# Summing the squares of the value products with one matmul: fold to 64 partitions, stack rounded part and remainder

## The chip, the cores and the metric

The kernel runs on one core of a Trainium2 chip. The metric is the device time of one execution in microseconds (us), the median of several. The engines are TensorE (PE; its weight loads are PEld), VectorE (DVE), ScalarE (ACT), GpSimd (POOL) and SyncE (SP), which here only issues transfers.

## The reference, cut to what matters

The reference is a two-layer decoder trunk on 1024 tokens of width 1024. Layer 0 is a retention mixer, layer 1 differential attention with 16 heads. What the change touches is the end of layer 1: the attention output of each head, 128 wide, gets an RMS norm over those 128 values.

```python
attn = probs[:, :, 0] - lam * probs[:, :, 1]
...
out = rmsnorm(out, subln_g, eps=GN_EPS) * (1.0 - lambda_init)
y = out.transpose(0, 2, 1, 3).reshape(B, S, D_INNER)
gated = jax.nn.silu(g.astype(jnp.float32)) * y
return gated.astype(w_out.dtype) @ w_out
```

So for each head and each token the sum of 128 squares is needed. 

## The kernel before, in words

**Precision.** Every large matmul works on a rounded part (type fp32r) and a remainder, so a product is three matmuls: high x high, high x low, low x high. ACT rounds (a cast) and DVE or POOL subtracts to get the remainder.

**Layer 1.** `attention_layer` goes through 16 heads and, in each, through 8 blocks of 128 queries in the order 6, 2, 3, 7, 4, 0, 1, 5: 128 steps. In a step PE makes the logits of the next block (L752, L755). DVE finds row maxima (L780, L782, L783), ACT takes exponentials (L785), and DVE combines the two softmaxes into A (L788, L789, L791). PE transposes A (L809), ACT casts it (L812), DVE subtracts for the remainder (L813). After every second block, `values` multiplies V with the transposed weights of two blocks (L823 to L825) into one half of a PSUM bank `ob`: 128 partitions are the head's 128 value dimensions, 256 columns are two blocks of queries. There are 16 x 4 = 64 such value products.

**The squares.** Behind each value product ACT squares it (L831) and casts the square (L832), DVE subtracts for the remainder (L833), and a further DVE instruction makes the gated product `go` (L837 or L839). Later `square_sum` issues the transfer of `go` (L844), lets PE sum over partitions with a matrix of ones, once for the rounded part and once for the remainder (L845, L846), into the other half of the bank, and stores row 0 of it (L848, L849). The bank has one buffer. When a batch of heads (0 to 7, 8 to 11, 12 to 15) is complete, `row_scales` reads the sums back and makes the norm's factors; `finish` multiplies them into the stored products on POOL (L733) in later steps, for the first two batches.

**What sets the order.** PE's order is the program's order (a manual schedule). To fill PE's waits, the projections of later heads come as a generator, `filler`, in steps of about 0.65 us, and a counter `clk["pe"]` adds up estimated PE time. `fill_until(t)` pulls filler up to a time, with allowances from `SLACK` for what the other engines must do in between; `fill_total` spreads the filler over the steps, so its total is fixed. `ready_o` is the point after which a square sum may be issued: the counter after the value product plus `SLACK["sq"]`. It is issued in the next step, behind that step's transposes; at the end of the first two batches it is issued in the same step; after the last value product there is no filler left. ACT, DVE and POOL take their instructions from a list scheduler that goes by priority and by estimated readiness; the softmax, the casts of the transposes and the squares have raised priority. On the chip each of these engines runs its list in order. POOL also subtracts for the remainders of the weights (L83 and, for some of the output weights, L94).

Of the kernel before, what the change touches and what calls it, by code (L numbers as in the profile page):

```python
# [10 lines left out]
F32 = mybir.dt.float32  # L11
F32R = mybir.dt.float32r
I32 = mybir.dt.int32
AF = mybir.ActivationFunctionType
# [5 lines left out]
P = 128  # L20
# [8 lines left out]
NE = 16  # L29
NEG = -1.0e30  # L30
PRIO = 600
SLACK = {'base': 3.4, 'wide': 4.4, 'turn': 2.0, 'av': 1.6, 'sq': 2.0, 'qk': 1.2}
START_T = (("T", 1), ("R", 1))
MXB = 1
AHEAD = 2
# [11 lines left out]
def _f32(ap):  # L47
    return ap.bitcast(F32)


class _Trunk:
# [523 lines left out]
    def attention_layer(self, HR, QR, pmm, ws0, slots):  # L575
        nc, io = self.nc, self.io
        with ExitStack() as es:
# [8 lines left out]
            wk = self.pool(es, "l1w")  # L586
# [10 lines left out]
            def v_(h, kb, lo):  # L597
                return QR[:, 10 + 2 * (h % 3) + lo, kb * P:(kb + 1) * P]

            L, U = slice(0, 64), slice(64, 128)  # L600
# [96 lines left out]
            def fill_until(t):  # L697
                while clk["pe"] < t and pull():
                    pass
# [5 lines left out]
            def need(*key):  # L705
                while key not in done and pull():
                    pass
                assert key in done, key

            def batch(h):  # L710
                return next((b, h - h0, h1 - h0) for b, (h0, h1) in enumerate(BATCHES) if h < h1)
# [103 lines left out]
            def values(h, j):  # L815
                ath, atl = ats.pop((h, j))
                nk = 2 * j + 2
                ob = psm.tile([P, 512], F32, tag="AV", name="ps_o")
                o = ob[:, 0:256]
                for kb in range(nk):  # L820
                    last = kb == nk - 1
                    c0 = P if last else 0
                    nc.tensor.matmul(o[:, c0:], v_(h, kb, 0), ath[:, kb, c0:], start=(kb == 0), stop=False)  # L823
                    nc.tensor.matmul(o[:, c0:], v_(h, kb, 0), atl[:, kb, c0:], start=False, stop=False)
                    nc.tensor.matmul(o[:, c0:], v_(h, kb, 1), ath[:, kb, c0:], start=False, stop=last)  # L825
                clk["pe"] += nk * 0.327
                sq = wk.tile([P, 256], F32, tag="sq", name="sq")
                sqh = wk.tile([P, 256], F32R, tag="sqh", name="sqh")
                sql = wk.tile([P, 256], F32R, tag="sql", name="sql")
                with self.tc.high_priority(offset=PRIO):  # L830
                    nc.scalar.activation(sq, o, AF.Square)  # L831
                    nc.scalar.copy(sqh, sq)  # L832
                    nc.vector.tensor_sub(sql, sq, _f32(sqh))  # L833
                go = wk.tile([P, 256], F32, tag="go", name="go", bufs=2)
                if h < LATE:
                    sg = sgs[h][j // 2][:, (j % 2) * 256:(j % 2) * 256 + 256]
                    nc.vector.scalar_tensor_tensor(go, o, self.subg, sg, op0=ALU.mult, op1=ALU.mult)  # L837
                else:
                    nc.vector.tensor_scalar(go, o, self.subg, None, op0=ALU.mult)  # L839
                return ob, sqh, sql, go  # L840

            def square_sum(h, j, ob, sqh, sql, go):
                b, hh, nh = batch(h)
                nc.scalar.dma_start(self.g1r[b][2 * j:2 * j + 2, :, hh, :].rearrange("t p q -> p t q"), go.rearrange("p (t q) -> p t q", t=2))  # L844
                nc.tensor.matmul(ob[:, 256:512], self.ones, sqh, start=True, stop=False)  # L845
                nc.tensor.matmul(ob[:, 256:512], self.ones, sql, start=False, stop=True)  # L846
                ssr = wk.tile([1, 256], F32, tag="ssr", name="ssr")
                nc.vector.tensor_copy(ssr, ob[0:1, 256:512])  # L848
                nc.scalar.dma_start(self.ssd[b][2 * j:2 * j + 2, hh:hh + 1, :].rearrange("t a q -> a t q"), ssr.rearrange("a (t q) -> a t q", t=2))  # L849
# [34 lines left out]
            for s, (h, i) in enumerate(seq):  # L884
# [4 lines left out]
                if nxt is not None:  # L889
# [3 lines left out]
                    need("qk", seq[min(s + AHEAD, len(seq) - 1)][0])  # L893
                    fill_until(ready - SLACK["qk"])
                    Ss = logits(*nxt)
                    nready = clk["pe"] + SLACK["base"] + SLACK["wide"] * (nxt[1] + 1) / 8.0
                fill_until(ready)
# [12 lines left out]
                if i >= 4:  # L910
                    fill_until(t_done + SLACK["turn"])
                    attn_t(h, i, A, 1)
# [4 lines left out]
                if pend is not None:  # L917
                    fill_until(ready_o)
                    square_sum(*pend)
                    pend = None  # L920
                if i % 2 == 1:
                    need("v", h // 2)
                    if h < LATE:
                        need("g", h)
                    fill_until(t_done + SLACK["av"])
                    pend = (h, i // 2) + values(h, i // 2)
                    ready_o = clk["pe"] + SLACK["sq"]
                    if i == ORDER[-1] and h + 1 in (BATCHES[0][1], BATCHES[1][1]):
# [11 lines left out]
            if pend is not None:  # L940
                square_sum(*pend)
# [140 lines left out]
```

## Time and profile before

| | |
|---|---|
| median of three runs | 2182.5 us (2181.49 to 2183.46) |
| the profiled execution's own time | 2179.38 us |
| its span, first to last instruction | 2177.6 us |
| mean granted clock of TensorE | 0.997 |
| instructions | 31046 |

The page of the profile gives each engine's busy time over the span, then groups of instructions by line. A group's row has the number of instructions, the busy time, the mean duration and the idle time of the engine just in front of them with what ended it. A timeline row has the start, the duration, the engine and line, the operation and the tiles it writes and reads, and in brackets the idle time in front of it and its releaser. [...]

### The profile page before, as it was taken

The numbers are of one execution on the slowest core, as the hardware profiler recorded it, in microseconds if no ns is written. First come the engines' busy times: TensorE is split into PE (matmuls) and PEld (weight loads), VectorE is DVE, ScalarE is ACT, GpSimd is POOL, SyncE is SP. The second block draws the span as 40 slices with busy tenths as digits, with TensorE's granted clock in tenths as the row PEclk, the third lists the DMA queues.
The fourth block names the chain that finished last, engine by engine and source line by source line (L and its number), as shares of the span: only waits on it lengthen the run. The fifth ranks groups of instructions, "written<-read, shape, count | busy, mean of one in ns | idle before, by whom it ended". The sixth has DMA issues, their size and how long they took to land.

```text
span 2177.6 us, 31046 instructions
## 1 busy us (share of the span) xinstructions
PE 2132.8 (98%) x11861; PEld 1790.8 (82%) x11861; DVE 1283.4 (59%) x3155; ACT 851.6 (39%) x1638; POOL 429.3 (20%) x246
## 2 busy tenths in 40 slices
PE   8999999999999999999999999999999999999998
PEld 7888988898897888787888888888787878877776
DVE  6254344334437438646777666767766777776644
ACT  4121221122123333335455555554545555554321
POOL 2332501511512000121111111111133111211300
PEclk9999999999999999999999999999999999999999
DMA  4112112111213545311111111111244113334743
GB/s 167 62 39 68 57 39 73 47 54 54 64 57 99 179 155 174 113 48 42 49 37 42 49 40 42 39 38 43 84 135 136 47 38 95 112 104 146 257 150 134
DMA packets 98916, 185.48 MB, mean 85 GB/s; under 512 B 8848, under 2 KB 51024, under 8 KB 98640
## 3 DMA queue, kind: packets, MB, share of 16 engines
q1 hardware_dynamic: 63824, 166.50, 23.6%
q10 hardware_dynamic: 34944, 17.01, 2.6%
q8 instruction: 93, 1.52, 0.3%
q14 instruction: 55, 0.45, 0.1%
HBM read 147.67 MB, written 38.95 MB: 86 GB/s over the span
## 4 chain that ended last, share of the span: by engine, by line
PE 92%; DVE 3%; issue 1%; ACT 1%; DMA 1%; POOL 0%; ACTq 0%; DVEq 0%; POOLq 0%
PE ps_mm L158 6%; PE ps_mm L157 6%; PE ps_mm L159 5%; PE ps_mm L215 5%; PE ps_mm L122 5%; PE ps_mm L124 5%; PE ps_mm L123 5%; PE ps_mm L217 5%; PE ps_mm L216 5%; PE ps_t L809 3%; PE ps_ret L396 3%; PE ps_s L752 3%; PE ps_mm L650 3%; PE ps_mm L651 3%; PE ps_mm L652 3%; PE ps_mm L167 3%
## 5 line engine op out<-in xcount | busy, mean ns | idle before, releaser
L83 POOL TENSOR_TENSOR w_l<-w_raw,w_h 128x1024 fp32r<-128x1024 f32 x112 | 271.2, 2427 | 1168.8 <-ACT w_h L82 1165.3
L785 ACT ACTIVATE e<-ps_s,nm 128x896 f32<-128x896 f32 (+7 forms) x256 | 189.8, 742 | 103.4 <-DVE nm L783 93.8
L215 PE MATMUL ps_mm<-RB,w_h 128*128 128x512 f32 x512 | 209.4, 409 | 0.4 <-ACT RB L150 0.4
L157 PE MATMUL ps_mm<-RA,w_h 128*128 128x512 f32 x512 | 203.9, 398 | 1.2 <-DVE sg L426 1.1
L158 PE MATMUL ps_mm<-RA,w_h 128*128 128x512 f32 x512 | 204.6, 400 | 0.0
L216 PE MATMUL ps_mm<-RB,w_h 128*128 128x512 f32 x512 | 201.9, 394 | 1.0 <-DVE RB L151 1.0
L217 PE MATMUL ps_mm<-RB,w_l 128*128 128x512 f32 x512 | 202.5, 395 | 0.0
L159 PE MATMUL ps_mm<-RA,w_l 128*128 128x512 f32 x512 | 201.9, 395 | 0.0
L812 ACT CAST ath<-ps_t 128x512 fp32r<-128x512 f32 (+1 forms) x192 | 91.9, 479 | 227.0 <-PE ps_t L809 217.5
L780 DVE TENSOR_REDUCE mx<-ps_s 128x1 f32<-128x640 f32 (+2 forms) x192 | 119.5, 622 | 78.7 <-PE ps_s L755 74.4
L82 ACT CAST w_h<-w_raw 128x1024 fp32r<-128x1024 f32 x112 | 117.6, 1050 | 123.2 <-PE ps_mm L158 39.0
L650 PE MATMUL ps_mm<-w_h,RB 128*128 128x256 f32 x512 | 147.4, 288 | 0.0
L169 PE MATMUL ps_mm<-w_h,RA 128*128 128x256 f32 x512 | 146.1, 286 | 0.0
L167 PE MATMUL ps_mm<-w_h,RA 128*128 128x256 f32 x512 | 145.3, 285 | 0.5 <-ACT RA L150 0.5
L168 PE MATMUL ps_mm<-w_l,RA 128*128 128x256 f32 x512 | 145.2, 285 | 0.1
L111 DVE TENSOR_TENSOR g_l<-w_raw,g_h 128x1024 fp32r<-128x1024 f32 x60 | 82.7, 1378 | 105.7 <-ACT g_h L110 105.6
L651 PE MATMUL ps_mm<-w_l,RB 128*128 128x256 f32 x512 | 143.6, 280 | 0.0
L652 PE MATMUL ps_mm<-w_h,RB 128*128 128x256 f32 x512 | 143.6, 280 | 0.0
L110 ACT CAST g_h<-w_raw 128x1024 fp32r<-128x1024 f32 x60 | 63.0, 1051 | 172.2 <-PE ps_mm L123 126.4
L157 PEld LDWEIGHTS ps_mm<-RA,w_h 128*128 128x128 f32 x512 | 96.1, 188 | 24.5 <-DVE sg L426 1.6
L217 PEld LDWEIGHTS ps_mm<-RB,w_l 128*128 128x128 f32 x512 | 96.1, 188 | 23.7
L159 PEld LDWEIGHTS ps_mm<-RA,w_l 128*128 128x128 f32 x512 | 96.2, 188 | 22.3
(211 smaller groups left out, 5392.7 us busy)
## 6 DMA issues: line engine op xcount, KB each, us to landing
w_raw<-in_wn SPq DMA_DIRECT2D x64, 512.0 KB
w_raw<-in_wv SPq DMA_DIRECT2D x32, 512.0 KB
w_raw<-in_wo SPq DMA_DIRECT2D x32, 512.0 KB
w_raw<-g SPq DMA_DIRECT2D x32, 512.0 KB
w_raw<-g1f SPq DMA_DIRECT2D x24, 512.0 KB
xt<-in_x SPq DMA_DIRECT2D x16, 512.0 KB
w_raw<-in_wg SPq DMA_DIRECT2D x16, 512.0 KB
g<-go ACTq DMA_DIRECT2D x32, 256.0 KB
```

Of the source, the lines that this page charges most:

```text
L83: nc.gpsimd.tensor_sub(l, raw, _f32(h))
L157: nc.tensor.matmul(ps, wh[:, k], region[:, kt, cols], start=(kt == 0), stop=False)
L158: nc.tensor.matmul(ps, wh[:, k], region[:, 8 + kt, cols], start=False, stop=False)
L159: nc.tensor.matmul(ps, wl[:, k], region[:, kt, cols], start=False, stop=(kt == KT - 1))
L167: nc.tensor.matmul(ps, region[:, kt, cols], wh[:, k], start=(kt == 0), stop=False)
L215: nc.tensor.matmul(ps, wh[:, k], HR[:, kt, tok], start=(kt == 0), stop=False)
L216: nc.tensor.matmul(ps, wh[:, k], HR[:, 8 + kt, tok], start=False, stop=False)
L217: nc.tensor.matmul(ps, wl[:, k], HR[:, kt, tok], start=False, stop=(kt == KT - 1))
L650: nc.tensor.matmul(ps[:, t, :], HR[:, kt, cols], wh[:, k], start=(kt == 0), stop=False)
L651: nc.tensor.matmul(ps[:, t, :], HR[:, kt, cols], wl[:, k], start=False, stop=False)
L652: nc.tensor.matmul(ps[:, t, :], HR[:, 8 + kt, cols], wh[:, k], start=False, stop=(kt == KT - 1))
L785: nc.scalar.activation(e[:, 0:n], S[:, 0:n], AF.Exp, bias=nm, accum_out=(s0 if m == 0 else s1))
```

## The change

The product's 128 partitions are squared in two instructions of 64 partitions each, the second half into a tile of its own that lies on the first 64 partitions. POOL adds the two halves. ACT casts the 64-partition sum into partitions 0 to 63 of a 128-partition tile `sqs`, and DVE writes the remainder into partitions 64 to 127. One matmul with ones then sums all 128 partitions, rounded part and remainder together. `SLACK["sq"]` goes from 2.0 to 3.2.

```diff
-SLACK = {'base': 3.4, 'wide': 4.4, 'turn': 2.0, 'av': 1.6, 'sq': 2.0, 'qk': 1.2}
+SLACK = {'base': 3.4, 'wide': 4.4, 'turn': 2.0, 'av': 1.6, 'sq': 3.2, 'qk': 1.2}
...
-                sq = wk.tile([P, 256], F32, tag="sq", name="sq")
-                sqh = wk.tile([P, 256], F32R, tag="sqh", name="sqh")
-                sql = wk.tile([P, 256], F32R, tag="sql", name="sql")
+                sq = wk.tile([64, 256], F32, tag="sq", name="sq")
+                sqb = wk.tile([64, 256], F32, tag="sqb", name="sqb")
+                sqs = wk.tile([P, 256], F32R, tag="sqs", name="sqs")
                 with self.tc.high_priority(offset=PRIO):
-                    nc.scalar.activation(sq, o, AF.Square)
-                    nc.scalar.copy(sqh, sq)
-                    nc.vector.tensor_sub(sql, sq, _f32(sqh))
+                    nc.scalar.activation(sq, o[L], AF.Square)
+                    nc.scalar.activation(sqb, o[U], AF.Square)
+                    nc.gpsimd.tensor_add(sq, sq, sqb)
+                    nc.scalar.copy(sqs[L], sq)
+                    nc.vector.tensor_sub(sqs[U], sq, _f32(sqs[L]))
...
-                return ob, sqh, sql, go
-
-            def square_sum(h, j, ob, sqh, sql, go):
+                return ob, sqs, go
+
+            def square_sum(h, j, ob, sqs, go):
...
-                nc.tensor.matmul(ob[:, 256:512], self.ones, sqh, start=True, stop=False)
-                nc.tensor.matmul(ob[:, 256:512], self.ones, sql, start=False, stop=True)
+                nc.tensor.matmul(ob[:, 256:512], self.ones, sqs, start=True, stop=True)
```

`L` and `U` are the partitions 0 to 63 and 64 to 127.

## Rows read from the trace of the kernel before

**Rows 1.** The page, part 1: busy time, share of the span, instructions.

```profile
PE 2132.8 (98%) x11861; PEld 1790.8 (82%) x11861; DVE 1283.4 (59%) x3155; ACT 851.6 (39%) x1638; POOL 429.3 (20%) x246
```

**Rows 2.** Busy time by stretch: length, PE, PEld, DVE, ACT, POOL, clock, DMA share, GB/s.

```profile
980.00:2003.00 1023.00, 1003.31 (x5915) 837.87 (x5913) 728.76 (x1932) 535.87 (x1147) 176.17 (x83) 1.00 0.22 67
```

**Rows 3.** PE's waits from 980 to 2010: total us, times, longest.

```profile
PE ps_t L809 <- DVE e L791: 4.1, 5, 2.0
```

**Rows 4.** Timeline, DVE and PE: first and last tight transposes of 14.

```profile
1050.89 1.28 DVE L791 SCALAR_TENSOR_TENSOR e<-e,arr 128x1024 f32<-128x1024 f32 x1
...
1052.40 0.60 PE L809 MATMUL ps_t<-ident,e 128*128 128x128 f32 x4
...
1994.50 1.02 DVE L791 SCALAR_TENSOR_TENSOR e<-e,arr 128x768 f32<-128x768 f32 x1
...
1995.80 0.60 PE L809 MATMUL ps_t<-ident,e 128*128 128x128 f32 x4
```

**Rows 5.** Timeline of PE around one square sum.

```profile
1316.10 0.37 PE L845 MATMUL ps_o<-sqh,ones 128*128 128x256 f32 x1
1316.30 0.28 PE L846 MATMUL ps_o<-sql,ones 128*128 128x256 f32 x1
1316.42 0.28 PE L650 MATMUL ps_mm<-w_h,RB 128*128 128x256 f32 x1
```

**Rows 6.** Timeline of ACT, DVE and PE from one Square to the next transposes.

```profile
1570.37 0.59 ACT L223 ACTIVATE RA<-ps_mm 64x512 fp32r<-64x512 f32 x1
1570.99 0.39 ACT L831 ACTIVATE sq<-ps_o 128x256 f32<-128x256 f32 x1
...
1571.27 1.11 ACT L785 ACTIVATE e<-ps_s,nm 128x1024 f32<-128x1024 f32 x1
...
1572.36 0.41 ACT L832 CAST sqh<-sq 128x256 fp32r<-128x256 f32 x1
...
1573.47 1.29 DVE L791 SCALAR_TENSOR_TENSOR e<-e,arr 128x1024 f32<-128x1024 f32 x1
...
1574.90 0.63 PE L809 MATMUL ps_t<-ident,e 128*128 128x128 f32 x4 [0.80 <-DVE e L791]
...
1575.56 0.59 ACT L812 CAST ath<-ps_t 128x512 fp32r<-128x512 f32 x1 [2.79 <-PE ps_t L809]
```

**Rows 7.** Timeline of ACT: first and last of 13 exponentials between Square and cast.

```profile
1014.86 0.89 ACT L785 ACTIVATE e<-ps_s,nm 128x768 f32<-128x768 f32 x1
...
1992.46 0.90 ACT L785 ACTIVATE e<-ps_s,nm 128x768 f32<-128x768 f32 x1
```

**Rows 8.** Waits of ACT and DVE from 980 to 2010.

```profile
ACT e L785 <- DVE sql L833: 3.7, 7, 0.5
...
DVE go L837 <- ACT sq L831: 24.8, 29, 2.4
```

**Rows 9.** Groups by line, POOL: count, busy us, mean ns, idle before, releasers.

```profile
L83 POOL TENSOR_TENSOR w_l<-w_raw,w_h 128x1024 fp32r<-128x1024 f32 x112 | 271.2, 2427 | 1168.8 <-ACT w_h L82 1165.3 <-PE ps_t L147 3.1
```

**Rows 10.** One line of layer 0, POOL: ns min/median/max, first and last start.

```profile
L314 POOL TENSOR_TENSOR ya<-ya,yb x32: 732/742/1194, 84.6 to 591.4; 128x256 f32<-128x256 f32 x32
```

**Rows 11.** Timeline of DVE and PE at the end of the first batch.

```profile
1481.83 1.65 DVE L833 TENSOR_TENSOR sql<-sq,sqh 128x256 fp32r<-128x256 f32 x1
...
1483.57 0.28 PE L845 MATMUL ps_o<-sqh,ones 128*128 128x256 f32 x1
```

**Rows 12.** Timeline of ACT and PE behind the last value product.

```profile
2001.77 0.38 ACT L831 ACTIVATE sq<-ps_o 128x256 f32<-128x256 f32 x1 [2.85 <-PE ps_o L825]
...
2002.82 0.35 PE L845 MATMUL ps_o<-sqh,ones 128*128 128x256 f32 x1 [1.45 <-DVE go L839]
```

**Rows 13.** Timeline of POOL, DVE and PE around the longest L791.

```profile
1638.06 2.37 POOL L83 TENSOR_TENSOR w_l<-w_raw,w_h 128x1024 fp32r<-128x1024 f32 x1
...
1638.43 3.08 DVE L791 SCALAR_TENSOR_TENSOR e<-e,arr 128x1024 f32<-128x1024 f32 x1
...
1641.66 0.63 PE L809 MATMUL ps_t<-ident,e 128*128 128x128 f32 x4 [1.98 <-DVE e L791]
```

## The prediction

> **What bounds the kernel now.** The totals come first: TensorE (PE) is busy in 98% of the span [rows 1]; nothing else passes 59% except the weight loads that overlap PE. The change lies in the attention layer alone, so the stretch from the first Square to the last square sum is read next: in 1023 us PE is busy for 1003.31 at a granted clock of 1.00 and idle for 19.7, POOL is busy for 176.17, that is 17% [rows 2]. The largest of PE's waits there is that of the transposes L809 for the finished softmax, L791: 4.1 us in five [rows 3]. So a PE instruction taken away is worth its issue time, and what is put on ACT, POOL and DVE costs nothing unless a softmax chain grows that PE already waits for. How close that is shows in the distance from the end of L791 to its transposes: in 14 of 128 softmaxes it is under 0.3 us (the first and the last are shown) [rows 4]; in those 14, 11%, PE takes the data as it comes.
>
> **Removed on PE.** 16 heads with four value products each make 64 folds, and each loses one matmul of 128x256. Its price is not the 0.28 us of its row but the distance to the next start: L846 at 1316.30, L650 at 1316.42 [rows 5]. The 0.20 us from L845 to L846 there follows transposes in front of L845 and stays. 64 x 0.12 = **-7.7 us**.
>
> **Added on ACT.** Square reads half the partitions, but of the same 256 columns; ACT takes 0.59 us for 64x512 (L223) and 0.59 for 128x512 (L812) [rows 6], so halving partitions saves nothing and each Square stays at 0.38: 64 x 0.38 = 24 us more work on an engine with 535.87 busy in 1023 [rows 2]. The second Square starts 0.28 us behind the first, as L785 does behind L831 [rows 6]. What stands behind it moves by that. In 13 of 64 folds an exponential stands between Square and cast (one in full, and the exponentials of the first and the last) [rows 6, 7]; three of these lead to a tight transpose (1052.40, 1574.90, 1995.80) [rows 4, 6]. Those three pay 3 x 0.28 = **+0.8 us**. Bounds: 0, and 13 x 0.28 = 3.6 if all pay. The two half casts and subtractions keep their columns and so their 0.41 and 0.42; DVE gains nothing.
>
> **Taken out of ACT's way.** Where the cast runs right behind Square, the exponential comes after it; in seven folds it even waits for the remainder subtraction, 3.7 us in all [rows 8]. The new cast can't start until the add is done, so these exponentials get ahead of the subtraction. Three of the seven lead to a tight transpose; each gets back 3.7/7 = 0.53 less the 0.28 by which go (L837, which starts when Square ends, 24.8 us of DVE waits [rows 8]) and the nm behind it move: 3 x 0.25 = **-0.7 us**. Bounds: -3.7 and +0.8 (three tight ones lose 0.28 instead).
>
> **Added on POOL.** No row shows a 64x256 add; the nearest is layer 0's 128x256, 0.74 us [rows 10]. The halves side by side don't shorten it if ACT's rows are a guide, so 0.74 is taken, with half of that and the 1.19 maximum as ends. The Square-to-remainder chain grows by 0.28 + 0.74 and about 0.04 for the hop, 1.06 us. The square sum itself has room: in program order the next step's logits and transposes lie between it and its values. The close cases are the ends of two batches, where it is issued at once; the first has its remainder done at 1483.48 and L845 at 1483.57 [rows 11]. There the slack goes from 2.0 to 3.2, about two filler steps of 0.65, which covers the 1.06. The filler is a fixed amount and only comes earlier, so the slack is costed at nothing; without that cover each such end would cost about 1 us.
>
> **POOL's queue.** POOL works in order. It is busy 17% of the time, so some 11 of 64 adds find it occupied, mostly by the 2.43 us subtraction of L83 [rows 2, 9]; behind L733, which waits for transfers, it could be longer. Half of 2.43 is 1.2, so 13 us are lost there in all, and they sit in the cast on ACT and the remainder on DVE, which have exponentials, L812 and L813 behind them. With 11% of softmaxes tight, 13 x 0.11 = **+1.4 us**. Bounds: 0, and 13 if every delay reaches PE. No DMA is moved; ACT's issues of go and of the sums (L844, L849) stay behind the same results, the latter up to 1.06 us later, and nobody but the batch end reads them.
>
> **The end of the layer.** The last fold has no filler behind it: values end, Square at 2001.77, L845 at 2002.82, then the scales [rows 12]. This chain lies open and grows by 1.06: **+1.1 us** (0.7 to 1.5 with the ends of the add).
>
> **Sum:** -7.7 + 0.8 - 0.7 + 1.4 + 1.1 = -5.1 us. Against the profiled execution (2179.38 us, of which the span is 2177.6) that gives 2174.3; that execution is 3.1 us under the median of the runs, 2182.5, so the forecast is 2182.5 - 5.1 = **2177.4 us**, 0.23% faster. A measurement of this kernel can tell 0.2%, 4.4 us, from no change.
>
> **Rival 1: POOL's add meets DVE at the memory (no change).** The trace shows such a meeting: the L791 that began at 1638.43 took 3.08 us, while another of its shape took 1.29; POOL ran L83 from 1638.06 for 2.37, and PE waited 1.98 us [rows 6, 13]. [...] If an add lies in the way of L791 in the half of the 14 tight softmaxes that follow a fold, each costs 0.74: 7 x 0.74 = 5.2, in place of the three softmax terms: -7.7 + 1.1 + 5.2 = -1.4, **2181.1 us**. For it: DVE is busy 71% of the stretch [rows 2]. Against it: the add would run from 0.7 to 1.4 us behind Square, and L791 at 1573.47 starts 2.5 us behind its own [rows 6].
>
> **Rival 2: ACT and DVE stand still behind the add (slower).** If the cast is placed in ACT's order ahead of the next exponential or L812, ACT stands for the whole 1.06 us, and DVE at the remainder likewise: 64 x 1.06 = 68 us. It turns into a slower kernel when 7.7 - 1.1 + 4.4 = 11.0 us of it reach PE, 16% of 68. At a fifth, 13.6: **2189.5 us**. For it: both queues are in order, and in the seven folds above an exponential waits for a remainder already [rows 8]. Against it: the order is made with readiness in view; in 13 folds it already puts the exponential ahead of a cast that waits only for Square.
>
> **Rival 3: the change does less than it says.** PE could spend the freed 0.12 us waiting, since the removed matmul lies between the logits and the transposes of the next softmax and covers part of the wait. That hits the tight ones only: 14 x 0.12 = 1.7 off the gain, 2179.1, no measurable change.
>
> **How the numbers follow.** Forecast case, 0.46: faster. Rival 1: 0.27, rival 3: 0.10, both no change. Rival 2: 0.17, slower. The range begins at -9 (all of -7.7 and 1.1, and some 2 us of PE's present waits for softmaxes shortened), 2173.5, and ends at +6, 2188.5, inside rival 2, of which the upper half is left out. The forecast's own range is 2173.5 to 2178.1.
>
> **What would show it.** Right: PE with 64 fewer matmuls and about 7.5 us less time from issue to issue; PE's idle time in the stretch at 19.7 plus about 2.6; two Squares of 0.38; POOL's adds near 0.74 us with waits of about 1.2 in some ten cases; at the end of the layer about 2.1 us from the second Square's start to the matmul. Wrong: casts with long waits for POOL and a longer sum of waits of L809 for L791, L812 or L813 (rival 2); L791 or L83 with much longer maxima in folds (rival 1). Adds far over 1.2 us, or the exponentials behind the cast on ACT, would make the prediction wrong.

## The result, and the profile after it

The changed kernel takes **2193.66 us** (median of four runs, 2192.33 to 2196.21) where the kernel before took 2181.99 in the same series: a ratio of **1.0055 [1.0043, 1.0067]**, 11.7 us or 0.55% slower. The forecast, 2177.4, has the wrong sign, and the time lies above its range. The profiled execution took 2194.57 us; its span is 2192.5 and the mean granted clock 0.993 (before: 2179.38, 2177.6, 0.997).

The page, part 1, of the changed kernel; it answers to [rows 1]:

```profile
PE 2134.7 (97%) x11797; PEld 1786.2 (81%) x11797; DVE 1300.8 (59%) x3155; ACT 873.7 (40%) x1702; POOL 477.2 (22%) x310
```

PE has its 64 matmuls fewer, and yet 1.9 us more busy time. The stretch from the first square sum to the last tells why. Columns: length, PE, PEld, DVE, ACT, POOL, granted clock, DMA share, GB/s. The kernel before:

```profile
990.60:2003.10 1012.50, 993.60 (x5862) 829.93 (x5860) 720.26 (x1912) 529.52 (x1136) 176.17 (x83) 1.00 0.22 67
```

The changed kernel, the same stretch, and below it 6.7 us of it just behind the end of the first batch:

```profile
992.00:2015.70 1023.70, 993.43 (x5799) 824.14 (x5797) 735.73 (x1912) 551.38 (x1199) 225.23 (x146) 0.99 0.22 67
...
1491.30:1498.00 6.70, 5.24 (x16) 3.76 (x16) 5.07 (x21) 1.83 (x5) 0.00 (x0) 0.50 0.29 85
```

The stretch grew by 11.2 us. PE's idle time is length less busy time: 1012.50 - 993.60 = 18.9 before, 1023.70 - 993.43 = 30.3 after, **+11.4**. Its busy time is unchanged (-0.2) although 64 x 0.12 = 7.7 us of issue are gone, so some 7.5 us of other busy time took their place. A good part of it lies where the granted clock is 0.50, the lower clock of this text. PE of the changed kernel on the way into that stretch:

```profile
1487.77 0.40 PE L609 MATMUL ps_mm<-RB,w_h 128*128 128x512 f32 x1
1488.01 0.40 PE L610 MATMUL ps_mm<-RB,w_l 128*128 128x512 f32 x1
1490.71 0.39 PE L847 MATMUL ps_o<-sqs,ones 128*128 128x256 f32 x1 [2.31 <-DVE sqs L835]
...
1495.21 0.63 PE L609 MATMUL ps_mm<-RB,w_h 128*128 128x512 f32 x1
1495.64 0.63 PE L610 MATMUL ps_mm<-RB,w_l 128*128 128x512 f32 x1
```

From L609 to L610 it is 0.24 us ahead of the wait of 2.31 and 0.43 behind it: here the granted clock is 0.50 from 1491.3 us for 6.8, and PE loses time a second time. From 980 us to the output projection the trace has four such stretches after (from 1491, 1938, 1993 and 2017 us) and one before (from 1928), of 3.4 us each but for the first. Between the two square sums PE is busy at the lower clock for 12.2 us, before for 3.3; at 0.43 in place of 0.24 a matmul, the difference costs some 4 us, an estimate. Another 2.6, also an estimate, fit the waits themselves: PE waits 39 times in place of 23, and a matmul with a wait behind it is busy for its whole 0.28 us, not for the 0.12 to the next start [rows 5].

The clock doesn't part the kernels, however. With only the second matmul left out (the first experiment), PE's stretch is this:

```profile
992.50:1998.50 1006.00, 987.90 (x5798) 823.88 (x5796) 721.13 (x1912) 530.31 (x1136) 178.38 (x83) 0.99 0.22 68
```

There the mean granted clock is 0.99, as in the changed kernel, and yet that kernel is faster by the whole price of its matmuls. Its idle time is 18.1 us, as before: what sets the changed kernel apart is the waits.

The removed matmul itself did what it should. The changed kernel around one square sum:

```profile
1320.65 0.37 PE L847 MATMUL ps_o<-sqs,ones 128*128 128x256 f32 x1
1320.86 0.28 PE L650 MATMUL ps_mm<-w_h,RB 128*128 128x256 f32 x1
```

From the sum to L650 it is 0.21 us, where it was 0.32 [rows 5]. **The idle time** is in these waits of PE in the changed kernel (total us, times, longest):

```profile
PE ps_o L847 <- DVE sqs L835: 6.5, 4, 2.7
PE ps_t L809 <- DVE e L791: 5.7, 10, 1.1
PE ps_t L809 <- DVE atl L813: 5.5, 7, 1.1
PE ps_t L809 <- DVE nm L783: 3.3, 3, 1.7
```

Two of the same waits in the kernel before; the other two are in [rows 3] and [rows 12]:

```profile
PE ps_t L809 <- DVE atl L813: 3.2, 4, 1.2
PE ps_t L809 <- DVE nm L783: 1.0, 1, 1.0
```

The square sum itself now waits for the remainder, 6.5 us in four (before, 1.5 in one, and for `go` [rows 12]); the transposes wait for the softmax in ten cases where they did in five [rows 3]. The four rows grew from 9.8 to 21.0 us, nearly all of the 11.4. All four waits end with DVE. What happens there is seen in one ordinary fold of the changed kernel (ACT, DVE, POOL, PE in order of time):

```profile
1180.26 0.38 ACT L831 ACTIVATE sq<-ps_o 64x256 f32<-64x256 f32 x1 [0.23 <-PE ps_o L825]
1180.65 0.38 ACT L832 ACTIVATE sqb<-ps_o 64x256 f32<-64x256 f32 x1
1181.05 1.12 ACT L785 ACTIVATE e<-ps_s,nm 128x1024 f32<-128x1024 f32 x1
1181.06 0.48 DVE L839 SCALAR_TENSOR_TENSOR go<-ps_o,subg,sg 128x256 f32<-128x256 f32 x1 [0.56 <-ACT sqb L832]
1181.11 0.74 POOL L833 TENSOR_TENSOR sq<-sq,sqb 64x256 f32<-64x256 f32 x1 [10.80 <-ACT sqb L832]
...
1182.16 0.39 ACT L834 CAST sqs<-sq 64x256 fp32r<-64x256 f32 x1
...
1182.74 1.28 DVE L791 SCALAR_TENSOR_TENSOR e<-e,arr 128x1024 f32<-128x1024 f32 x1
1183.58 2.68 POOL L83 TENSOR_TENSOR w_l<-w_raw,w_h 128x1024 fp32r<-128x1024 f32 x1 [1.74 <-ACT w_h L82]
1184.06 2.49 DVE L835 TENSOR_TENSOR sqs<-sq,sqs 64x256 fp32r<-64x256 f32 x1
...
1186.58 0.56 DVE L780 TENSOR_REDUCE mx<-ps_s 128x1 f32<-128x384 f32 x1
...
1189.72 0.55 PE L809 MATMUL ps_t<-ident,e 128*128 128x128 f32 x3 [1.71 <-DVE nm L783]
```

The same fold in the kernel before, DVE and POOL:

```profile
1179.14 0.42 DVE L833 TENSOR_TENSOR sql<-sq,sqh 128x256 fp32r<-128x256 f32 x1
...
1180.39 2.62 POOL L83 TENSOR_TENSOR w_l<-w_raw,w_h 128x1024 fp32r<-128x1024 f32 x1 [13.77 <-ACT w_h L82]
```

Read it from the top: the exponential runs while POOL adds, as forecast; the cast comes at once behind it. But the subtraction now lies behind L791, after the start of POOL's L83, and takes **2.49 us in place of 0.42**; the row maximum of the next softmax (L780) stands behind it on DVE, and PE waits 1.71 us. Before, the subtraction was over 0.8 us before L83 began. In the changed kernel ten of 64 subtractions take over 0.6 us, before four.

The end of the first batch in the changed kernel (before: [rows 11]):

```profile
1484.34 2.89 POOL L83 TENSOR_TENSOR w_l<-w_raw,w_h 128x1024 fp32r<-128x1024 f32 x1 [10.46 <-ACT w_h L82]
...
1485.29 0.38 ACT L832 ACTIVATE sqb<-ps_o 64x256 f32<-64x256 f32 x1
...
1487.19 0.73 POOL L833 TENSOR_TENSOR sq<-sq,sqb 64x256 f32<-64x256 f32 x1
1488.03 2.35 POOL L83 TENSOR_TENSOR w_l<-w_raw,w_h 128x1024 fp32r<-128x1024 f32 x1
1488.11 0.41 ACT L834 CAST sqs<-sq 64x256 fp32r<-64x256 f32 x1
...
1488.71 1.94 DVE L835 TENSOR_TENSOR sqs<-sq,sqs 64x256 fp32r<-64x256 f32 x1
```

The same place in the kernel before, ahead of [rows 11]:

```profile
1480.29 2.90 POOL L83 TENSOR_TENSOR w_l<-w_raw,w_h 128x1024 fp32r<-128x1024 f32 x1 [29.11 <-ACT w_h L82]
1480.97 0.39 ACT L831 ACTIVATE sq<-ps_o 128x256 f32<-128x256 f32 x1 [0.75 <-PE ps_o L825]
```

Before, POOL's L83 held up the subtraction alone (1.65 us), and from the end of Square (1481.36) to the sum (1483.57) it was 2.2 us. After, POOL hits twice: the add stands 1.5 us behind one L83 (second Square done at 1485.67), and the subtraction runs beside the next. The sum comes at 1490.71, 5.0 us behind the second Square, and here the distance between the two traces, same PE instruction against same PE instruction, grows by about 4 us. Behind the last value product the sum comes 2.63 us behind the first Square's start; before it was 1.05 [rows 12]. The changed kernel there:

```profile
2013.04 0.38 ACT L831 ACTIVATE sq<-ps_o 64x256 f32<-64x256 f32 x1 [2.43 <-PE ps_o L825]
...
2015.20 0.42 DVE L835 TENSOR_TENSOR sqs<-sq,sqs 64x256 fp32r<-64x256 f32 x1 [0.88 <-ACT sqs L834]
2015.67 0.38 PE L847 MATMUL ps_o<-sqs,ones 128*128 128x256 f32 x1 [2.73 <-DVE sqs L835]
```

And the subtraction in the kernel before:

```profile
2002.63 0.42 DVE L833 TENSOR_TENSOR sql<-sq,sqh 128x256 fp32r<-128x256 f32 x1
```

Before, the first matmul needed of this chain the cast alone (the profile has it wait for `go`, a reader of the same bank): it starts at 2002.82 [rows 12], while the subtraction is at work. The one matmul of the changed kernel can't start before the subtraction is done.

The waits of ACT and DVE from 980 to 2010 us after the change, which answer to [rows 8], and POOL's add, which answers to [rows 10] (ns, min/median/max):

```profile
ACT sqs L834 <- POOL sq L833: 19.5, 13, 5.1
ACT e L785 <- DVE atl L813: 6.5, 7, 1.2
...
DVE go L839 <- ACT sqb L832: 26.3, 32, 2.2
```

```profile
L833 POOL TENSOR_TENSOR sq<-sq,sqb x64: 715/732/1704, 984.7 to 2013.9; 64x256 f32<-64x256 f32 x64
```

The exponentials no longer wait for the remainder subtraction, but longer for L813, 6.5 us in seven (before, 3.1 in three). The cast waits for POOL in 13 folds; these waits include the add itself. The add finds POOL busy in 11 folds, where it starts over 0.2 us behind its second Square, 16.4 us in all.

### The profile page after: what moved, and what is told of

Read it like the earlier page. It is cut to its first block, busy times and chain, and to the rows that moved or that the text cites. A ratio compares the mean times of both kernels' runs of the same rounds, so it can differ in the third digit from the quotient of the medians.

```text
span 2192.5 us, 31171 instructions
## 1 busy us (share of the span) xinstructions
PE 2134.7 (97%) x11797; PEld 1786.2 (81%) x11797; DVE 1300.8 (59%) x3155; ACT 873.7 (40%) x1702; POOL 477.2 (22%) x310
## 4 chain that ended last, share of the span: by engine, by line
PE 82%; DVE 6%; DMA 4%; ACT 2%; issue 2%; POOL 1%; ACTq 0%; SPq 0%; DVEq 0%; POOLq 0%
PE ps_mm L158 5%; PE ps_mm L157 5%; PE ps_mm L159 5%; PE ps_mm L215 5%; PE ps_mm L216 5%; PE ps_mm L217 5%; PE ps_mm L122 4%; PE ps_mm L123 4%; PE ps_mm L124 4%; PE ps_ret L396 3%; PE ps_t L809 3%; PE ps_mm L167 3%; PE ps_mm L169 3%; PE ps_mm L168 3%; PE ps_s L752 2%; PE ps_mm L650 2%
## 5 line engine op out<-in xcount | busy, mean ns | idle before, releaser
L83 POOL TENSOR_TENSOR w_l<-w_raw,w_h 128x1024 fp32r<-128x1024 f32 x112 | 273.5, 2446 | 833.7 <-ACT w_h L82 797.8
L216 PE MATMUL ps_mm<-RB,w_h 128*128 128x512 f32 x512 | 202.6, 396 | 1.0 <-DVE RB L151 1.0
L780 DVE TENSOR_REDUCE mx<-ps_s 128x1 f32<-128x640 f32 (+2 forms) x192 | 119.5, 622 | 74.5 <-PE ps_s L755 70.5
L650 PE MATMUL ps_mm<-w_h,RB 128*128 128x256 f32 x512 | 147.4, 288 | 0.0
L652 PE MATMUL ps_mm<-w_h,RB 128*128 128x256 f32 x512 | 143.6, 280 | 0.0
L833 POOL TENSOR_TENSOR sq<-sq,sqb 64x256 f32<-64x256 f32 x64 | 48.7, 762 | 390.6 <-ACT sqb L832 360.2
L809 PE MATMUL ps_t<-ident,e 128*128 128x128 f32 x576 | 102.1, 286 | 14.9 <-DVE e L791 5.7
```

The lines of the kernel that those rows point to most:

```text
L83: nc.gpsimd.tensor_sub(l, raw, _f32(h))
L216: nc.tensor.matmul(ps, wh[:, k], HR[:, 8 + kt, tok], start=False, stop=False)
L650: nc.tensor.matmul(ps[:, t, :], HR[:, kt, cols], wh[:, k], start=(kt == 0), stop=False)
```

## The experiments

The expectations call theories by letters: A (PE gives the matmul's time back), Q (queueing behind POOL), O (the chain lies open at the batch ends and in the last head), D (DVE's late subtraction beside POOL's long ones); T, S and others are told where they stand. All ratios are to the kernel before on the same chip, with their 95% interval. They are not the ratios of the two medians, and where a kernel's times scatter the two differ (most with the subtraction on POOL, 1.0022, where the medians give 1.0031).

### What the matmul is worth

Before, with the second matmul left out:

```diff
-                nc.tensor.matmul(ob[:, 256:512], self.ones, sqh, start=True, stop=False)
-                nc.tensor.matmul(ob[:, 256:512], self.ones, sql, start=False, stop=True)
+                nc.tensor.matmul(ob[:, 256:512], self.ones, sqh, start=True, stop=True)
```

> The kernel before with only the matmul of the remainder (L846) taken away; Square, cast and subtraction stay, and the remainder is left out of the sum. Theory A (PE gives the time back one for one): 64 x 0.12 = 7.7 us, 2174.3. Rival (the freed time becomes waiting for the next softmax): less than half of it, 2178 or more.

2174.53 us, 0.9964 [0.9951, 0.9977]: -7.9 us, against the 7.7 of the sum. Then the remainder left out altogether, with Square writing the rounded square:

```diff
-                    nc.scalar.activation(sq, o, AF.Square)
-                    nc.scalar.copy(sqh, sq)
-                    nc.vector.tensor_sub(sql, sq, _f32(sqh))
+                    nc.scalar.activation(sqh, o, AF.Square)
...
-                nc.tensor.matmul(ob[:, 256:512], self.ones, sqh, start=True, stop=False)
-                nc.tensor.matmul(ob[:, 256:512], self.ones, sql, start=False, stop=True)
+                nc.tensor.matmul(ob[:, 256:512], self.ones, sqh, start=True, stop=True)
```

> The kernel before with Square rounding straight into the matmul's type: cast, subtraction and the second matmul are gone, and the remainders of the squares are left out of the sum. If PE's issue time is all: 2174.5, like the run with one matmul. If the work on ACT and DVE (0.41 + 0.42 us per fold) holds up softmaxes as the added Square and add did: 3 us or more below that, 2171.5 or less.

2172.46, 0.9962 [0.9950, 0.9975]: the same within the intervals. So the cast and the subtraction cost the kernel before nothing that can be measured.

### The added work alone, in the kernel before

An unused second Square and an unused add on POOL:

```diff
+                sqx = wk.tile([64, 256], F32, tag="ssr", name="sqx")
...
+                    nc.scalar.activation(sqx, o[U], AF.Square)
+                    nc.gpsimd.tensor_add(sqx, sqx, sq[L])
```

> The kernel before with a second Square of 64 partitions on ACT and a 64x256 add on POOL in each fold, whose result nobody uses; both matmuls stay. Theory O (the time was lost because the chain from value product to square sum is longer where it lies open): no change, 2182 to 2183.5. Theory D/Q (the added work itself holds up ACT, DVE and POOL): most of the loss, +8 us or more, 2190.

2187.79, 1.0028 [1.0017, 1.0039], +6.1 us, between the marks of O and of D and Q. Without the add:

```diff
-                    nc.gpsimd.tensor_add(sqx, sqx, sq[L])
```

> The kernel before with the second Square of 64 partitions on ACT in each fold, unused; no POOL add. Splits the 5.7 us of the side load. ACT is the cause: 4 us or more over before, 2186. POOL's add (beside DVE) is the cause: 2 us at most, 2184.

2186.10, 1.0019 [1.0010, 1.0028], +4.1. And with the second Square reading the first one's result in SBUF in place of the PSUM bank:

```diff
-                    nc.scalar.activation(sqx, o[U], AF.Square)
+                    nc.scalar.activation(sqx, sq[U], AF.Square)
```

> The kernel before with a second Square of 64 partitions in each fold, unused, as in the run with the second Square alone (+4.1 us), but reading the first Square's result in SBUF and not the product's PSUM bank, so that go (L837, L839) on DVE starts behind the first Square again. If the loss comes from go being held behind the second reader of the bank: +1.5 us at most, 2183. If ACT's 0.38 us is the cause: +4 us again, 2186.

2184.36, 1.0009 [1.0000, 1.0017], +2.0. The two intervals overlap, so that half of the second Square's price is the bank and not ACT's time is likely but not shown. What the bank does to `go` is shown: the kernel with the PSUM read, then the one with the SBUF read, ACT and DVE in one fold.

```profile
1182.03 0.38 ACT L832 ACTIVATE sq<-ps_o 128x256 f32<-128x256 f32 x1 [1.01 <-PE ps_o L825]
1182.44 0.38 ACT L833 ACTIVATE sqx<-ps_o 64x256 f32<-64x256 f32 x1
1182.85 0.48 DVE L839 SCALAR_TENSOR_TENSOR go<-ps_o,subg,sg 128x256 f32<-128x256 f32 x1 [0.89 <-ACT sqx L833]
```

```profile
1178.71 0.38 ACT L832 ACTIVATE sq<-ps_o 128x256 f32<-128x256 f32 x1 [1.01 <-PE ps_o L825]
1179.13 0.48 DVE L839 SCALAR_TENSOR_TENSOR go<-ps_o,subg,sg 128x256 f32<-128x256 f32 x1 [0.49 <-ACT sq L832]
1180.22 0.42 ACT L833 ACTIVATE sqx<-sq 64x256 f32<-64x256 f32 x1
```

`go` reads the bank that Square reads, and starts behind its last ACT reader: 0.82 us behind the first Square's start in the one, 0.42 in the other. In all 64 folds of the kernel before and of the changed one `go` starts 0.03 us or more behind the end of the last Square. Why a reader waits for a reader is not shown.

### Undoing parts of the changed kernel

The add on DVE:

```diff
-                    nc.gpsimd.tensor_add(sq, sq, sqb)
+                    nc.vector.tensor_add(sq, sq, sqb)
```

> The changed kernel with the add of the halves on DVE instead of POOL (0.42 us more on DVE per fold, no POOL queue in the chain). Theory D/Q (POOL in the chain holds ACT's cast and sets DVE's subtraction beside L83): 5 us or more come back, 2188 or less. Theory O: the chain is only some 0.3 us shorter, 1 to 2 us come back, 2191.5 to 2193; if the DVE work counts, slower than the changed kernel.

2190.55, 1.0041 [1.0029, 1.0053]: -3 against the changed kernel, less than the intervals tell apart. The six folds where the chain lies open (the last of the first two batches, the four of the last head) done the old way, with two matmuls, the other 58 as in the change:

```diff
+                fold = h < DH - 1 and not (j == ORDER[-1] // 2 and h + 1 in (BATCHES[0][1], BATCHES[1][1]))
+                    if fold:
...
+                        nc.gpsimd.tensor_add(sq[L], sq[L], _f32(sql[L]))
...
+                    else:
+                        nc.scalar.activation(sq, o, AF.Square)
+                        nc.scalar.copy(sqh, sq)
+                        nc.vector.tensor_sub(sql, sq, _f32(sqh))
```

> The changed kernel, but the folds at the ends of the first two batches and in the last head (2 + 4 of 64) keep the old way with two matmuls. Theory O: the roughly 4 us of the first batch end and 6 of the last head come back, 2184 or less. Theory D (the remainder subtraction held by POOL's L83 in ordinary folds): at most 3 us come back, 2190 or more.

2188.36, 1.0029 [1.0019, 1.0039]: 5.7 us back (0.0055 - 0.0029 = 0.0026 of 2182). O holds for that part; 6.3 us of loss remain in folds that have cover. Giving the open ends more slack instead:

```diff
-SLACK = {'base': 3.4, 'wide': 4.4, 'turn': 2.0, 'av': 1.6, 'sq': 3.2, 'qk': 1.2}
+SLACK = {'base': 3.4, 'wide': 4.4, 'turn': 2.0, 'av': 1.6, 'sq': 6.0, 'qk': 1.2}
```

> The changed kernel with the allowance for the square sum at 6.0 instead of 3.2. Theory O: the two batch ends are covered, 3 to 4 us come back, 2190; the last head, which has no filler left, stays as it is. If the batch ends don't matter: 2193.7 within 1 us.

2191.48, 1.0051 [1.0039, 1.0064]: a miss, the larger number buys nothing that can be measured. The remainder subtracted on POOL, behind its own add:

```diff
-                    nc.vector.tensor_sub(sqs[U], sq, _f32(sqs[L]))
+                    nc.gpsimd.tensor_sub(sqs[U], sq, _f32(sqs[L]))
```

> The changed kernel with the remainder subtraction on POOL instead of DVE, so that DVE no longer stands in the chain. Theory D (DVE held at the subtraction, up to 2.5 us beside L83, in ordinary folds): 5 us or more come back, 2188.5 or less, though the open ends get longer by 0.3 us each or, behind L83, 2.4. If DVE is not the one: the changed kernel's 2193.7 or above.

2188.28, 1.0022 [1.0012, 1.0032], 7 us back by the ratios and 5.4 by the medians, though PE's wait for the remainder at the open ends is no shorter (its waits: `PE ps_o L847 <- POOL sqs L835: 7.5, 3, 3.1`). So what is won should lie in the folds with cover. Both steps together, the open folds the old way and POOL's subtraction in the 58 others:

```diff
-                        nc.vector.tensor_sub(sqh[U], sq[L], _f32(sqh[L]))
+                        nc.gpsimd.tensor_sub(sqh[U], sq[L], _f32(sqh[L]))
```

> Both partial cures at once: the six folds at open ends keep the old way, and in the other 58 the remainder is subtracted on POOL instead of DVE. If the open ends (5.3 us came back) and DVE's subtraction in ordinary folds (7 us came back) are separate parts of the loss: 2193.7 - 12.3 = 2181.4, level with before. If they are the same time counted twice: 2186 or more.

2180.50, 0.9992 [0.9982, 1.0002]: the parts add up, and what the matmuls gave is spent: the kernel comes out even. From the kernel with the six folds the old way, POOL's subtraction gives 8 us back (1.0029 to 0.9992). Two tries to save the bank's price with one full Square and an ACT copy of its upper half from SBUF, in the changed kernel and in the one just told:

```diff
-                    nc.scalar.activation(sq, o[L], AF.Square)
-                    nc.scalar.activation(sqb, o[U], AF.Square)
+                    nc.scalar.activation(sq, o, AF.Square)
+                    nc.scalar.copy(sqb, sq[U])
...
```

> The changed kernel with one Square of 128 partitions and an ACT copy of its upper half from SBUF in place of the second Square; the rest as changed. Same count of ACT instructions, go released 0.4 us earlier. If holding go matters: 3 us come back, 2190.5. If ACT's time does: 2193.7 within 1 us.

> The same, and the upper half copied from SBUF as in the run with the copy. If holding go is a third part: 3 us under the run before it, 2178.5, faster than before by 0.15%. If not: level with it, within 1 us.

2194.02, 1.0059 [1.0047, 1.0072], and 2182.46, 1.0001 [0.9993, 1.0010]: both misses. In the first of them DVE waits 20.1 us for `go` on L839 where it waited 26.3, and the kernel is no faster. The copy makes the chain as long as the second Square did; that this is why nothing was won is not shown.

### Is it the subtraction, or its lateness?

POOL's subtraction in the kernel before, in the 58 folds, with nothing else changed; and DVE's subtraction there put behind a POOL instruction of the add's size:

```diff
-                    nc.vector.tensor_sub(sql, sq, _f32(sqh))
+                    late = h == DH - 1 or (j == ORDER[-1] // 2 and h + 1 in (BATCHES[0][1], BATCHES[1][1]))
+                    (nc.vector if late else nc.gpsimd).tensor_sub(sql, sq, _f32(sqh))
```

> The kernel before with one thing changed: in the 58 folds with cover the remainder of the squares is subtracted on POOL instead of DVE; no second Square, no add, both matmuls. Theory D (what the subtraction on POOL gave back in the changed kernel, some 7 us, was the delay of DVE's subtraction behind POOL's add and beside L83): here there is no such delay to give back, since in the kernel before only 4 of 64 subtractions take over 1.3 us, so -1 to +1 us, about 2182. Rival (DVE's time as such is worth it: 58 x 0.42 = 24 us of work leave DVE, and some of it reaches PE): -4 us or more, 2178 or less.

```diff
+                    if not (h == DH - 1 or (j == ORDER[-1] // 2 and h + 1 in (BATCHES[0][1], BATCHES[1][1]))):
+                        nc.gpsimd.tensor_mul(sq[0:64], sq[0:64], self.onesq)
...
```

> The kernel before with one thing added: in the 58 folds with cover POOL multiplies the first 64 partitions of the square by ones, in place (64x256, the size of the changed kernel's add), between Square and cast, so cast and subtraction stand behind POOL as in the changed kernel. No second Square, both matmuls, the six late folds as before. Theory D: the delay of cast and subtraction costs 7 us in the changed kernel, and here the same, with about 2 us for the load of POOL's instruction: +7 to +10 us, 2189 to 2192. Rival (only the load costs, the place in the chain nothing): +2 us, 2184.

Without an add in front, POOL's subtraction costs 3 us (2184.37, 1.0015 [1.0007, 1.0024]), so DVE's time as such is not what it gave back in the changed kernel. But the delay alone costs little too: 2184.76, 1.0004 [0.9994, 1.0013], with a POOL instruction that is a little shorter than the add (median 0.61 us). D in its strong form, 7 us from the delay alone, falls. And ACT's share, with POOL making the cast behind its add in the kernel with the six open folds the old way:

```diff
-                        nc.scalar.copy(sqh[L], sq[L])
+                        nc.gpsimd.tensor_copy(sqh[L], sq[L])
```

> The changed kernel with the six late folds the old way (it took 2188.4), and in the 58 folds with cover POOL makes the cast right behind its add, in place of ACT. ACT then never stands at a cast behind POOL, DVE's subtraction still does. Theory D (what is lost in these folds is lost in DVE, behind a late subtraction): no gain, 2187 to 2190. Rival 2 of the prediction in its first half (ACT stands still at the cast and the exponentials and casts behind it come late): 4 us or more back, 2184 or less.

2193.27, 1.0049 [1.0036, 1.0061]: 4 us worse than with ACT's cast, where relief of ACT should have given 4 back. So ACT's standing at the cast is not seen to be the loss; POOL's cast brings a load of its own, and 13 subtractions take over 0.6 us there, against 9 with ACT's cast.

### A chain of kernels, one edit apart

The second Square joins the chain of the kernel before (58 folds); from that the second matmul is dropped; and on the other side the changed kernel with old open folds gets its slack back.

```diff
                     if not (h == DH - 1 or (j == ORDER[-1] // 2 and h + 1 in (BATCHES[0][1], BATCHES[1][1]))):
+                        nc.scalar.activation(sq[0:64], o[L], AF.Square)
                         nc.gpsimd.tensor_mul(sq[0:64], sq[0:64], self.onesq)
```

> The kernel before with the second Square and POOL's instruction put into the chain of the 58 folds with cover, and nothing else: Square of all 128 partitions, Square of the first 64 once more over it, POOL's multiply by ones in place (64x256), cast, subtraction, all of 128 partitions, two matmuls as before; the six late folds as before. By themselves the second Square cost 4 us and POOL's instruction in the chain 1 to 3. Theory T (threshold: each eats the same slack in front of PE, and only together they pass it): more than the sum, +11 to +14 us, 2193 to 2196, which is what the folds with cover cost in the changed kernel without the 7 us of their matmuls. Rival S (the costs add; what is missing lies in the stacked half tiles or the single matmul): +5 to +7 us, 2187 to 2189.

```diff
-                nc.tensor.matmul(ob[:, 256:512], self.ones, sqh, start=True, stop=False)
-                nc.tensor.matmul(ob[:, 256:512], self.ones, sql, start=False, stop=True)
+                late = h == DH - 1 or (j == ORDER[-1] // 2 and h + 1 in (BATCHES[0][1], BATCHES[1][1]))
+                nc.tensor.matmul(ob[:, 256:512], self.ones, sqh, start=True, stop=not late)
+                if late:
+                    nc.tensor.matmul(ob[:, 256:512], self.ones, sql, start=False, stop=True)
```

> The kernel with second Square and POOL's instruction in the chain (2185.7), and in the 58 folds with cover the second matmul dropped (the remainder of the square is computed and left out of the sum). If the removed matmul is worth the same with the longer chain in front of it: 58 x 0.12 = 7 us less, 2178 to 2180; then the 7 to 8 us between this kernel and the changed one with the late folds the old way (2188.4) lie in the stacking: half-tile cast and subtraction, or the one matmul that waits for the subtraction. If the removed matmul had covered waits that now show (rival 3 of the prediction, at full size): 0 to -2 us, 2184 to 2186, with PE's busy time 7 us shorter and its idle time longer by as much.

```diff
-SLACK = {'base': 3.4, 'wide': 4.4, 'turn': 2.0, 'av': 1.6, 'sq': 3.2, 'qk': 1.2}
+SLACK = {'base': 3.4, 'wide': 4.4, 'turn': 2.0, 'av': 1.6, 'sq': 2.0, 'qk': 1.2}
```

> The changed kernel with the six late folds the old way (2188.4), and SLACK of the square sum back from 3.2 to 2.0. If the larger slack, which takes filler out of the steps behind it, costs PE its cover there: 4 us or more back, 2184 or less. If the place of the filler is all one there: 2187 to 2190.

Measured: 2185.68, 1.0021 [1.0012, 1.0030]; 2180.97, 0.9994 [0.9985, 1.0003]; 2183.70, 1.0006 [0.9997, 1.0015]. T (the costs pass a threshold together) falls, S (they add) holds. With the kernels above they make a path from the kernel before to the changed one; each step is a difference of two ratios times 2182, uncertain by about 3 us (2 for the first), so that the stacking's 2.6 can't be told from nothing:

| step | ratio to | us |
|---|---|---|
| second Square and POOL's instruction in the chain, 58 folds | 1.0021 | +4.6 |
| second matmul dropped in them | 0.9994 | -5.9 |
| half tiles stacked: the one matmul needs the subtraction | 1.0006 | +2.6 |
| slack 2.0 to 3.2 | 1.0029 | +5.0 |
| six open folds the new way | 1.0055 | +5.7 |

PE between first and last square sum in four of these kernels (columns as above): second matmul dropped; stacked with slack 2.0; stacked with slack 3.2.

```profile
992.10:2002.30 1010.20, 987.01 (x5804) 822.47 (x5801) 726.94 (x1912) 545.60 (x1193) 214.80 (x140) 1.00 0.22 68
```

```profile
990.70:2008.00 1017.30, 990.11 (x5804) 823.50 (x5802) 740.98 (x1912) 549.99 (x1193) 222.35 (x140) 1.00 0.22 67
```

```profile
993.00:2009.50 1016.50, 991.36 (x5803) 824.38 (x5801) 739.98 (x1912) 549.75 (x1193) 221.45 (x140) 0.99 0.22 67
```

Idle time goes from 18.9 us before to 23.2, 27.2 and 25.1, and to 30.3 in the changed kernel; in these single traces the stacking is worth 4 us of it, the open folds 5. The last two rows also show a limit. PE's order in these two kernels differs only at the two batch ends (one step of L608 to L610 and three of L650 to L652 come ahead of the sum), and in this pair the stretch is not longer with the larger slack. Their profiled executions are 2.9 us apart, of which 2.3 come ahead of the first square sum (at 990.7 and 993.0), where PE's order is still the same. So that the slack costs something follows from the ratios of 9 and 11 runs on two chips; where it costs, and whether 5 us is its own size, stays **open**. The kernel with POOL's subtraction has the slack of 3.2 too and comes out even (0.9992), level with the one whose sum doesn't need the remainder (0.9994). So the stacking and the slack together, 7.6 us, are lost only with the subtraction on DVE, or POOL's subtraction wins something else of that size; no run has it with the slack of 2.0.

## Why the prediction was wrong

The sum gave -5.1 us, the path gives +12.0. Of the 17 between them, 4.6 lie in the six open folds (+5.7, where the sum had +1.1 for the last one and nothing for the batch ends), 5.0 in the slack (nothing in the sum), 3.1 in the second Square and POOL's instruction in the chain (+4.6, where the sum had 0.8 - 0.7 + 1.4), 2.6 in the stacking (no term) and 1.8 in the matmuls; each part is uncertain by about 3 us. **The steps that failed are the slack "costed at nothing" with a chain that grows by 1.06 and is covered, and the price of the second Square**; the delay that the longer chain hands to DVE was left out of the step on POOL's queue.

**Removed on PE** (-7.7): right. 0.9964 is -7.9 alone, and -5.9 for 58 behind the longer chain. Rival 3, that PE waits the freed time away, is not seen beyond the intervals.

**Added on ACT** (+0.8, bounds 0 to 3.6): the duration was right, 0.38 each, the price was not: +4.1 alone. The second Square starts 0.39 us behind the first (1180.26 and 1180.65), not 0.28, which was read off an exponential behind a Square. The step looked at ACT's own queue (three tight exponentials). It named that `go` starts when Square ends [rows 8], but did not ask which Square: `go` starts behind the second one (1181.06, that one done at 1181.03), and `nm` of the next softmax stands behind it on DVE. With the read from SBUF +2.0 are left, a difference within the intervals.

**Taken out of ACT's way** (-0.7): the 3.7 us of exponentials behind the subtraction [rows 8] went as told, but no gain shows: seven exponentials wait for L813 now, 6.5 us (three before, 3.1), on the DVE queue in which the late subtraction lies. No run prices this step by itself.

**Added on POOL**: the add is as forecast (median 0.73, 0.72 to 1.70), and 64 partitions cost what 128 did [rows 10]. The failed part is "the slack is costed at nothing". At the first batch end the larger slack brought one filler step of three matmuls ahead of the sum, 0.7 us, not two; and it met a chain that grew from 2.2 to 5.0 us behind the last Square, not by 1.06: L83 stood in front of the add and then beside the subtraction, and the lower clock (0.50 from 1491.3 us) came on top. The text had a price for lost cover, about 1 us per end; the measured one is some 4 at that end. With the last head the six open folds cost 5.7. And the larger slack was not free but, by the ratios, a loss, whose place stays open.

**POOL's queue** (+1.4, bounds 0 to 13): the add's wait for POOL came about as told, 16.4 us in 11 folds against 13 in 11. The step left out the second meeting: a subtraction that comes a microsecond or more later falls on other work of POOL's, and ends 0.28 us behind it (2.49 us in place of 0.42 in the fold above); DVE's 64 subtractions take 40.4 us in place of 33.4. What that costs is shown at the batch end. In the folds with cover it is shown only in part: POOL's subtraction gives 8 us back there, but the delay alone costs 0.9 in the kernel before, and the kernel with only the second matmul left out has eight subtractions over 0.6 us and is the faster by all its matmuls. A held subtraction costs where PE stands behind it; by which way it does so in the folds with cover stays open.

**The end of the layer** (+1.1): 1.6, 2.63 against 1.05 from Square to sum, and behind it 3.4 us at a granted clock of 0.50, from 2017 us. The step priced the chain from Square to remainder alone. But before, the first matmul started ahead of the remainder's end, and the one matmul that is left waits for it.

**Rivals.** Rival 1 had POOL and DVE in each other's way, but on L791 and on the add; it is the remainder subtraction beside L83 that takes 2.49 us in place of 0.42. That they meet at the memory is not shown. Rival 2 had the sign and the DVE half of the place; its measure, a fifth of 68 us reaching PE (+13.6 before the matmul's -7.7), comes near the idle time of +11.4, but by luck: it let ACT stand in all 64 folds, and the cast waits for POOL in 13. No case had the clock in it, some 4 us in the two profiles.

## What to carry to other kernels

Lengthening an in-order chain has to be priced by where its links land, not only by how long they are: look at what each late instruction will now run beside, and who stands behind it. A matmul of 0.12 us buys little: here all 64 gave 7.9 us, the second Square alone took 4.1, and the six places where the chain has no filler behind it took 5.7, so such places are better left the old way. Ask who else reads what an added instruction reads: behind a second Square of the same bank `go` started 0.82 us behind the first in place of 0.42. And look at the granted clock behind a wait of PE: behind the 2.31 us at the batch end it was 0.50 for 6.8 us, with 0.43 us from matmul to matmul in place of 0.24.

## What the runs showed of the hardware

**The subtractions on DVE that start beside a POOL instruction end behind it.** Every subtraction of the squares that took over 0.6 us, ten in the changed kernel and four before, overlaps an instruction of POOL's (L83, L94 or L733) that began earlier, and ends 0.28 us behind that one's end: 1183.58 + 2.68 = 1186.26 and 1184.06 + 2.49 = 1186.55 in the fold above, 1488.03 + 2.35 = 1490.38 and 1488.71 + 1.94 = 1490.65 at the batch end. In the kernel with only the delay added it is the same, POOL and DVE there:

```profile
1180.19 2.43 POOL L83 TENSOR_TENSOR w_l<-w_raw,w_h 128x1024 fp32r<-128x1024 f32 x1 [1.98 <-ACT w_h L82]
1180.31 2.60 DVE L835 TENSOR_TENSOR sql<-sq,sqh 128x256 fp32r<-128x256 f32 x1
```

So the price in these rows is not a slower rate but the rest of POOL's instruction; L83 and L94 take 2.35 to 3.37 us in the changed kernel, and the longest of its subtractions 2.58. What the two engines share there is not shown.

**The lower clock comes and goes.** The changed kernel has 3.4 us at a granted clock of 0.50 from 914.5 us; the kernel before, with the same order of PE up to there, has 1.00. Against it the changed kernel's PE is 0.4 us early ahead of that stretch and 1.1 us late behind it: 1.5 us. Nor does a wait settle it: both traces have PE's wait at L216 there, of 1.04 and 1.03 us, and only the one has the lower clock; with the wait of 2.31 and 2.33 us at L824 late in the layer (to 1937.22, before to 1927.95) both have it. Executions of one kernel differ as well: in twelve of the one with the longer chain and the second matmul dropped the mean granted clock goes from 0.993 to 0.998 and the time from 2175.88 to 2185.49 us. Single traces therefore can't price edits of a few us; that took repeated executions.

**Half the partitions cost as much.** Square of 64x256 takes 0.38 us as that of 128x256 did [rows 6], cast and subtraction 0.41 and 0.42 (medians), again as before.
